# First output projection of a hybrid decoder block: convolution features in seven products, heads plain

## Chip, cores and metric

The kernel runs on one core of one Trainium2 chip. The metric is device microseconds (us) of the whole kernel, lower is better. Three runs of the kernel before gave 2041.8, 2042.85 and 2043.69 us, median 2042.85 us.

## The reference, cut to what matters

One decoder block over 2048 positions of width 1024 in float32: norm, one input projection, two mixers side by side, one output projection with residual, norm, a gated feed-forward part with residual, norm.

```python
proj = rmsnorm(x, norm1_g[l]) @ w_in[l]
p_q, p_k, p_v, p_g, p_a, c_b, c_c, c_h = jnp.split(proj, splits, axis=-1)
...
o = rmsnorm(gla_chunked(q, k, v, log_a), gla_norm_g[l]) 
o_gla = (o * silu(p_g)).reshape(bsz, seq, GLA_WIDTH)
o_conv = c_b * causal_depthwise_conv(c_c * c_h, conv_w[l])
mixed = jnp.concatenate([o_gla, o_conv], axis=-1) @ w_out[l]
x = x + mixed
h2 = rmsnorm(x, norm2_g[l])
x = x + (silu(h2 @ w_ffn_gate[l]) * (h2 @ w_ffn_up[l])) @ w_ffn_down[l]
```

The change lies in `mixed`: a product of 2048 x 1024 features (512 of gated linear attention, here "the heads", and 512 of the convolution) with a 1024 x 1024 matrix.

## The kernel before, in words

**Number format and products.** Features stand on the 128 partitions and positions in the free dimension, in four blocks `b` of 512. Each operand is split into two float32r parts, a high part made by ScalarE (L194) and a low part made by VectorE as the difference (L195); the helper `split` does both. A product step is then three matmuls of 128x512: high by high, high by low, low by high (L484 to L486 in `product_step`).

**Units.** The input projections and the feed-forward part work in units of a 2 x 2 scheme of Strassen and Winograd: two feature halves by two position blocks, seven products in place of eight. The list `PRODUCTS` names them: A11 B11, S1 T1, S2 T2, A12 B21, S3 T3, S4 B22, A22 T4, where the A's, S's are weights or their sums and the B's, T's operands or their differences. The results are accumulated in PSUM banks (`mm`) and by copies (`copied`, ScalarE, L530) and additions (`plus`, VectorE, L518) in tiles of SBUF. The operands T3, B22 and T4 (`WHOLE`) are stored as they are and split only when due, in the middle of a unit (`due`). Weights come raw from DRAM and are split into tiles `wq`, of which there are four buffers.

**Stages.** First input projection (blocks 0 and 1, `in_proj(0)`, to about 270 us), second one (blocks 2 and 3, `in_proj(1)`), then the output projection of blocks 0 and 1 (`out_proj(0)`, about 555 to 663 us) and that of blocks 2 and 3 (`out_proj(1)`), then the feed-forward part, twice. In `in_proj` the last units make the convolution; its result `y` (a tile of the pool `tp`, nine buffers that many purposes share) is split at once, and `hi` and `y` are stored in DRAM (`s_mix`). The recurrence of the heads (`gla_half`) runs as a background generator: `tick`, called between products, takes a step of it, so that its chunks are spread over the second input projection and the first output projection. The last step of a chunk transposes (`ot`, L1231), scales (`osb`, L1232), splits and stores (`s_gla`); the split is put behind the last copy and the last addition recorded (`behind(last_out + last_plus)`). The other generators hang on `tick` too: `ahead` takes a step at one tick in four.

**The output projection.** `out_proj(half, ops)` takes 16 operand pairs (8 k of 128 features by 2 blocks; k 0 to 3 the heads, 4 to 7 the convolution), all loaded ready split by `build_mix`. It makes four passes over `d0`, each for two rows `e` of 128 output features: four banks, and for each k, e and block j three matmuls (L1273, L1274, L1276). Behind a pass, four additions on VectorE of the residual `y` (L1298), four stores, four squares on ScalarE (L1254) and their sums on VectorE (L1255).

**What sets the order.** A scheduler orders the instructions of each engine ahead of time; every engine then takes its queue in order. All loads and stores are issued by SyncE (L148 and L151) in one order, and each DMA also waits for the landing of the eighth before it, since there are eight lanes. The operand pool `opp` has 28 buffers.

Of the kernel before, what the change touches and what calls it, by code (L numbers as in the profile page):

```python
# [16 lines left out]
ALU = mybir.AluOpType  # L17
# [36 lines left out]
def tile_hymba_block(ctx, tc, x, xt, win, wa, wgu, wout, wffn, wdown, wdown_first, small, out):  # L54
# [59 lines left out]
    s_mix = [[dram.tile([P, 2, PB], F32, name=f"sm{b}_{k}") for k in range(4)] for b in range(NB)]  # L114
    s_gla = [dram.tile([P, HEADS, 2, PB], F32, name=f"sgla{b}") for b in range(NB)]
    s_act = [
        [
# [279 lines left out]

    def weight_quarter(src):

        n = src.shape[-1]  # L400
# [7 lines left out]
        split(src, h[:, 0, :], h[:, 1, :])  # L408
        catch_up()
        return h  # L410

# [5 lines left out]
        return raw  # L417

    def unit_weights(src, raw=None, between=()):
        raw = raw_weights(src) if raw is None else raw  # L420
# [6 lines left out]
        n = src.shape[-1]  # L427
        a11, a12, a22, a21 = [raw[:, i, :] for i in range(4)]
        s1 = rawp.tile([P, PB], F32, name="s1", tag="s1", bufs=1)[:, 0:n]
# [24 lines left out]
        return w  # L454
# [585 lines left out]
    def forget_gate(b, i, z, em, dn, el):  # L1040
# [15 lines left out]
        dve.tensor_tensor(dn[:, i, :], em[:, i, :], el[:, i, :], ALU.mult)  # L1056
        store(s_d[b][i][:], t2[:])

    def in_proj(half, ops, raw=None, between=(), rest=None):
        def units():  # L1060
            if half == 0:
# [15 lines left out]
        for i0 in (0, 2):  # L1077
# [179 lines left out]
    def build_mix(half):  # L1257
        def pair(b, k):
            return load_pair(s_gla[b][:, k] if k < HEADS else s_mix[b][k - HEADS])

        return [[pair(2 * half + j, k) for j in range(2)] for k in range(KD)]

    def out_proj(half, ops, ahead=None, rest=None):
        ssq = []
        ws = chain.from_iterable(plain_weights(wout[u], 4) for u in range(4))
        for d0 in range(0, KD, 2):
            o = {(e, j): bank() for e in range(2) for j in range(2)}
            for k in range(KD):
                for e in range(2):
                    wh, wl = next(ws)  # L1270
                    for j in range(2):
                        m = ops[k][j]
                        pe.matmul(o[e, j][:], wh, m[:, 0, :], start=k == 0, stop=False)  # L1273
                        pe.matmul(o[e, j][:], wh, m[:, 1, :], start=False, stop=False)  # L1274
                    for j in range(2):
                        pe.matmul(  # L1276
                            o[e, j][:], wl, ops[k][j][:, 0, :], start=False, stop=k == KD - 1
                        )
# [6 lines left out]
                if half:  # L1285
                    for _ in range(1 if d0 == KD - 2 else 2):
                        next(rest if d0 == KD - 2 else ahead, None)
                tick()
            if d0 == 0:
                ssq += [  # L1290
# [391 lines left out]
    in_proj(0, ops, raw, between, rest)  # L1682
    drain_background()
    ops = load_pairs(s_h1)
    background.extend([pause(3), hastened(gla_half(0), 14), gate(1, ops)])
# [5 lines left out]
    ssq = out_proj(1, build_mix(1), h2_first(ssq, h2), h2_rest(h2))  # L1691
    ahead.append(h2_ahead(ssq))
    mixing.close()
    bx[:] = [
# [112 lines left out]
```

## Time and profile before

| | |
|---|---|
| median of three runs | 2042.85 us |
| the profiled execution's own time | 2040.97 us |
| its span | 2039.2 us |
| TensorE busy in the span | 2019.6 us, 99% |
| VectorE, ScalarE busy | 1534.0 us (75%), 966.0 us (47%) |
| bytes moved | 422.51 MB, 207 GB/s in the mean |

A timeline row gives the start and the duration in us, engine, line, operation, destination <- source, the shape and the count; in brackets the idle time of the engine ahead of it and what ended that. PEld are TensorE's weight loads, SPq is SyncE's issuing queue. A row of windows gives the stretch, its length, then busy us and count for PE, PEld, VectorE (DVE), ScalarE (ACT) and POOL, the granted TensorE clock, the DMA share and GB/s. A row of waits gives engine, tile and line, what it waited for, and the total, the count and the longest in us. Group rows end with the idle time ahead of the group and what ended it.

### The profile page before, as it was taken

What the parts mean: (1) busy time and instruction counts of PE and PEld (TensorE: products, weight loads), DVE (VectorE), ACT (ScalarE), POOL (GpSimd) and SP (SyncE); (2) the same over time, 40 slices, a digit from 0 to 9 for tenths busy, and PEclk for the clock granted to TensorE, in tenths of its full rate; (3) what the DMA queues carried; (4) which work ended last, traced back from release to release, by engine and by line L of the source; (5) the groups of instructions that cost most, each with busy time, mean ns of one, the idle gap of its engine ahead of it and who ended that gap; (6) DMA issues with size and microseconds to landing.
All of it is one profiled execution on the core that took longest, in us unless ns stands there. A gap on an engine that the chain in (4) does not pass through costs nothing.

```text
span 2039.2 us, 26918 instructions
## 1 busy us (share of the span) xinstructions
PE 2019.6 (99%) x9299; PEld 1659.4 (81%) x9299; DVE 1534.0 (75%) x2763; ACT 966.0 (47%) x1915; POOL 10.3 (1%) x17
## 2 busy tenths in 40 slices
PE   9999999999999999999999999999999999999998
PEld 8788877887888788888888888887888888888886
DVE  7888967659744697777777688887777767778886
ACT  6664455656533344444444452334534444454345
POOL 0000000000000000000000000000000000000001
PEclk9999999999999999999999999999999999999999
DMA  7356885524675983546545576577444434486653
GB/s 263 119 202 222 290 299 172 163 74 158 247 245 173 373 293 134 192 151 217 181 145 191 215 287 249 187 276 279 161 165 170 161 144 170 174 331 223 248 217 129
DMA packets 190887, 422.51 MB, mean 207 GB/s; under 512 B 20032, under 2 KB 67360, under 8 KB 181280
## 3 DMA queue, kind: packets, MB, share of 16 engines
q1 hardware_dynamic: 190032, 420.15, 58.2%
q8 instruction: 73, 1.20, 0.2%
q10 hardware_dynamic: 720, 0.66, 0.1%
q14 instruction: 62, 0.51, 0.1%
HBM read 276.02 MB, written 144.70 MB: 206 GB/s over the span
## 4 chain that ended last, share of the span: by engine, by line
PE 94%; DMA 2%; DVE 2%; ACT 1%; issue 0%; SPq 0%; POOL 0%; POOLq 0%; ACTq 0%; DVEq 0%
PE mm L484 26%; PE mm L486 26%; PE mm L485 26%; PE mm L1273 3%; PE mm L1274 3%; PE mm L1276 3%; PE a_ps L1008 1%; PE mm L789 1%; PE mm L791 1%; PE o_ps L1181 1%; PE mm L790 1%; PE mm L1594 1%; PE sc L1156 1%; PE o_ps L1188 1%; DMA op<-shT 0%; PE kv L1196 0%
## 5 line engine op out<-in xcount | busy, mean ns | idle before, releaser
L484 PE MATMUL mm<-op,wq 128*128 128x512 f32 x2443 | 951.4, 392 | 7.2 <-ACT op L194 4.1
L485 PE MATMUL mm<-op,wq 128*128 128x512 f32 x2443 | 950.2, 390 | 0.5 <-DVE op L195 0.5
L486 PE MATMUL mm<-op,wq 128*128 128x512 f32 x2443 | 940.5, 390 | 0.3
L194 ACT ACTIVATE wq<-raw 128x512 fp32r<-128x512 f32 (+2 forms) x612 | 356.8, 588 | 590.1 <-PE mm L486 469.9
L484 PEld LDWEIGHTS mm<-op,wq 128*128 128x128 f32 x2443 | 459.0, 188 | 108.8 <-ACT op L194 5.4
L486 PEld LDWEIGHTS mm<-op,wq 128*128 128x128 f32 x2443 | 458.9, 188 | 96.5 <-DVE wq L195 1.1
L485 PEld LDWEIGHTS mm<-op,wq 128*128 128x128 f32 x2443 | 459.1, 188 | 96.1 <-DVE op L195 2.4
L195 DVE TENSOR_TENSOR wq<-raw,wq 128x512 fp32r<-128x512 f32 (+2 forms) x612 | 385.4, 635 | 173.5 <-ACT wq L194 171.9
L518 DVE TENSOR_TENSOR c<-mm,c 128x512 f32<-128x512 f32 x196 | 134.7, 687 | 81.6 <-PE mm L486 72.0
L518 DVE TENSOR_TENSOR y<-mm,y 128x512 f32<-128x512 f32 x185 | 126.6, 687 | 53.8 <-PE mm L486 53.2
L530 ACT ACTIVATE c<-mm 128x512 f32<-128x512 f32 x198 | 115.4, 589 | 34.7 <-PE mm L486 30.6
L436 DVE TENSOR_TENSOR raw<-raw 128x512 f32<-128x512 f32 (+2 forms) x182 | 113.3, 628 | 2.1
L194 ACT ACTIVATE wq<-s 128x512 fp32r<-128x512 f32 (+2 forms) x96 | 56.3, 587 | 108.8 <-PE mm L486 95.7
L1273 PE MATMUL mm<-op,wq 128*128 128x512 f32 x256 | 101.1, 397 | 0.1
L1274 PE MATMUL mm<-op,wq 128*128 128x512 f32 x256 | 100.0, 391 | 0.0
L1276 PE MATMUL mm<-op,wq 128*128 128x512 f32 x256 | 82.3, 390 | 0.0
L436 DVE TENSOR_TENSOR s<-raw 128x512 f32<-128x512 f32 (+2 forms) x91 | 57.3, 629 | 27.3 <-DMA raw<-in_wffn_dram 19.7
L195 DVE TENSOR_TENSOR op<-op 128x512 fp32r<-128x512 f32 x94 | 62.1, 683 | 4.0 <-ACT op L194 3.9
L195 DVE TENSOR_TENSOR wq<-s,wq 128x512 fp32r<-128x512 f32 (+2 forms) x96 | 60.8, 633 | 1.9 <-ACT wq L194 1.0
L194 ACT ACTIVATE op<-op 128x512 fp32r<-128x512 f32 x94 | 54.9, 621 | 8.0 <-DMA op<-sa_T 4.3
L436 DVE TENSOR_TENSOR raw<-s,raw 128x512 f32<-128x512 f32 (+2 forms) x91 | 57.3, 630 | 1.3
L1273 PEld LDWEIGHTS mm<-op,wq 128*128 128x128 f32 x256 | 48.1, 188 | 11.8 <-issue 1.4
(231 smaller groups left out, 1610.2 us busy)
## 6 DMA issues: line engine op xcount, KB each, us to landing
raw<-in_wffn_dram SPq DMA_DIRECT2D x44, 1024.0 KB, 6.4
sa_B<-so SPq DMA_DIRECT2D x47, 512.0 KB, 4.2
op<-sa_B SPq DMA_DIRECT2D x47, 512.0 KB, 6.8
raw<-in_win_dram SPq DMA_DIRECT2D x22, 1024.0 KB, 5.8
sa_T<-so SPq DMA_DIRECT2D x44, 512.0 KB, 4.4
op<-sa_T SPq DMA_DIRECT2D x44, 512.0 KB, 6.7
raw<-in_wdown_dram SPq DMA_DIRECT2D x24, 768.0 KB, 5.4
sx<-y SPq DMA_DIRECT2D x48, 256.0 KB, 3.9
```

The lines of the kernel that those rows point to most:

```text
L194: last_hi[:] = [act.activation(hi, src, AF.Copy)]
L195: last_lo[:] = [dve.tensor_tensor(lo, src, hi.bitcast(F32), ALU.subtract)]
L436: dve.tensor_tensor(*args)
L484: pe.matmul(o[:], wh, xh, start=first and k == 0, stop=False, skip_group_check=True)
L485: pe.matmul(o[:], wh, xl, start=False, stop=False, skip_group_check=True)
L486: return pe.matmul(o[:], wl, xh, start=False, stop=k == n - 1, skip_group_check=True)
L518: last_plus[:] = [dve.tensor_tensor(t[:], o[:], t[:], ALU.add)]
L530: last_out[:] = [act.activation(t[:], o[:], AF.Copy)]
L789: pe.matmul(acc[:], wq[:, 0, c], p[:, 0, :], start=first, stop=False)
L1273: pe.matmul(o[e, j][:], wh, m[:, 0, :], start=k == 0, stop=False)
L1274: pe.matmul(o[e, j][:], wh, m[:, 1, :], start=False, stop=False)
L1276: pe.matmul(o[e, j][:], wl, ops[k][j][:, 0, :], start=False, stop=k == KD - 1)
```

## The change

Only the first output projection (blocks 0 and 1) and what feeds it:

- `s_mix` of blocks 0 and 1 is stored whole; the split into `hi` and `y` falls away there (in the second half it stands as before, as `pair_out`).
- A new generator `conv_operands` hangs on `ahead` during the second input projection. After four pauses it takes, for each of two k, five steps: load four blocks of `s_mix` into small tiles, make four differences, split B11, T1, B21 and T2 and store both parts, store T3 and T4 whole, in new tiles of DRAM (`s_conv`).
- `mix_operands` loads 14 operands of the convolution (8 pairs, 6 whole) and 8 pairs of the heads.
- `first_out_proj` takes the place of `out_proj(0)`. Per pass it makes the weights of seven products of 256 columns (`unit_weights` with four quarters given: seven splits and four sums and differences) and two splits of 512 for the heads, then seven products of two product steps with an addition after each use, then the heads' matmuls, those of e = 0, j = 0 on top of the bank of A12 B21, and four additions. The rows of the residual are loaded a pass ahead.
- `out_proj` keeps the second output projection alone.

```diff
-                hi = tp.tile([P, PB], F32R, name="hi", tag="t")
-                split(y[:], hi[:], y[:].bitcast(F32R))
                 dst = s_mix[2 * half + j][i0 + r]
-                store(dst[:, 0, :], hi[:].bitcast(F32))
-                store(dst[:, 1, :], y[:])
+                if half:
+                    pair_out(y, dst)
+                else:
+                    store(dst[:], y[:])
...
+    def conv_operands():
...
+        yield from pause(4)
+
+        def divided(y, n, k):
+            with behind(last_out + last_plus):
+                pair_out(y, s_conv[n][k])
+
+        for k in range(2):
...
+            for y, src in (
+                (b11, s_mix[0][k]), (b12, s_mix[1][k]), (b22, s_mix[1][k + 2]), (b21, s_mix[0][k + 2]),
+            ):
+                load(y[:], src[:])
+            yield
+            t3 = tt("t3")
+            subtract(t3, b22, b12)
+            store(s_conv["T3"][k][:], t3[:])
+            subtract(b12, b12, b11)
+            divided(b11, "B11", k)
+            yield
+            subtract(b22, b22, b12)
+            divided(b12, "T1", k)
+            yield
...
+        for d0 in range(0, KD, 2):
+            raw = raw_weights(wout[d0 // 2]).rearrange("p a (b e c) -> p (a b) e c", e=2, c=P)
+            quads = [raw[:, k : k + 2, e, :] for e, k in ((0, 4), (0, 6), (1, 6), (1, 4))]
+            w = unit_weights(None, quads)
+            wh = [weight_quarter(raw[:, 0:HEADS, e, :]) for e in range(2)]
...
+            def plus(at, o):
+                last_plus[:] = [dve.tensor_tensor(y[at][:], o[:], y[at][:], ALU.add)]
+                last_out[:] = last_plus
+                all_plus.extend(last_plus)
+
+            oa = mul(0)
+            plus((0, 0), oa)
+            ob = mul(1)
+            plus((1, 1), ob)
+            due("T3")
+            tick()
+            mul(2, oa)
+            plus((0, 1), oa)
+            due("B22")
+            o = mul(3)
+            tick()
+            mul(4, oa)
+            plus((1, 1), oa)
+            due("T4")
+            mul(5, ob)
+            plus((0, 1), ob)
+            tick()
+            mul(6, oa)
+            plus((1, 0), oa)
+            tick()
+            following = residual(d0 + 2) if d0 + 2 < KD else None
+            for e in range(2):
+                po = [bank() if e or j else o for j in range(2)]
+                for k in range(HEADS):
+                    c = slice(k * P, (k + 1) * P)
+                    for j in range(2):
+                        for part in range(2):
+                            pe.matmul(
+                                po[j][:], wh[e][:, 0, c], heads[k][j][:, part, :],
+                                start=k + part == 0 and e + j > 0, stop=False,
...
-    ssq = out_proj(0, build_mix(0))
+    ssq = first_out_proj(residual(0), *mix_operands())
```

**Where instructions move.** ScalarE's order at the boundary of the two input projections, before; `hi` are the convolution's high parts, c11, c22 and c12 the copies of the last unit's results, the last row the first split of T3:

```order
L194 ACTIVATE hi_2816<-c22_2412 128x512
L194 ACTIVATE hi_2822<-c12_2437 128x512
L194 ACTIVATE wq_2901<-raw_2889 128x512
L194 ACTIVATE wq_2904<-raw_2889 128x512
L194 ACTIVATE hi_2828<-c11_2507 128x512
L530 ACTIVATE c11_2920<-mm_2907 128x512
L194 ACTIVATE wq_2922<-raw_2889 128x512
L530 ACTIVATE c22_2939<-mm_2926 128x512
L194 ACTIVATE wq_2941<-raw_2889 128x512
L530 ACTIVATE c12_2956<-mm_2907 128x512
L194 ACTIVATE wq_2958<-raw_2889 128x512
L194 ACTIVATE op_2865<-op_2865 128x512
```

The same place with the change, where L198 is the line of `split` and L542 that of the copies:

```order
L542 ACTIVATE c11_2902<-mm_2889 128x512
L198 ACTIVATE wq_2883<-raw_2871 128x512
L198 ACTIVATE wq_2886<-raw_2871 128x512
L198 ACTIVATE wq_2904<-raw_2871 128x512
L542 ACTIVATE c22_2921<-mm_2908 128x512
L198 ACTIVATE wq_2923<-raw_2871 128x512
L542 ACTIVATE c12_2938<-mm_2889 128x512
L198 ACTIVATE wq_2940<-raw_2871 128x512
L198 ACTIVATE op_2847<-op_2847 128x512
```

The three `hi` rows are gone and the copies come in the same order; c22 and c12 waited there for lanes of DMAs beside TensorE, and with the change wait for TensorE alone.

ScalarE's order at the end of the first output projection, before; `gt<-osb` is the high part of the last chunk of the heads, the `wq` are weights of the second output projection:

```order
L1213 ACTIVATE sq_6548,hsq_6545<-o_ps_6536 128x128
L200 ACTIVATE hl_6546<-hsq_6545 128x4
L201 ACTIVATE hy_6547<-hl_6546 128x4
L194 ACTIVATE wq_6746<-raw_6717 128x512
L194 ACTIVATE gt_6296<-osb_6559 128x512
L194 ACTIVATE wq_6803<-raw_6717 128x512
L1254 ACTIVATE q_6663<-y_6589 128x512
```

The same place with the change (`q` are the squares, L1272):

```order
L198 ACTIVATE wq_6669<-raw_6641 128x512
L205 ACTIVATE hy_6718<-hl_6717 128x4
L1272 ACTIVATE q_6791<-y_6536 128x512
L198 ACTIVATE wq_6873<-raw_6871 128x512
L198 ACTIVATE wq_6900<-raw_6871 128x512
L1272 ACTIVATE q_6796<-y_6540 128x512
L198 ACTIVATE gt_6448<-osb_6730 128x512
L198 ACTIVATE wq_6957<-raw_6871 128x512
```

Two weight splits and two squares now stand between the row of `hy` and the head's split, where one weight split stood; `wq_6900` takes the buffer of `wq_6663`, the weights of the last product.

TensorE's order at that place with the change: `ot` are the last chunk's transposes, mm_6672 the bank of the last product (weights `wq_6663`), mm_6799 and mm_6800 the heads' banks:

```order
L1249 MATMUL ot_6754<-ident_87,osb_6730 128x128 x3
L1386 MATMUL mm_6799<-op_5790,wq_6669 128x512 x2
L1386 MATMUL mm_6800<-op_5792,wq_6669 128x512 x2
L1392 MATMUL mm_6799<-op_5790,wq_6669 128x512
L1392 MATMUL mm_6800<-op_5792,wq_6669 128x512
L1386 MATMUL mm_6799<-op_5794,wq_6669 128x512
L496 MATMUL mm_6672<-op_5786,wq_6663 128x512
L497 MATMUL mm_6672<-op_5786,wq_6663 128x512
L498 MATMUL mm_6672<-op_5786,wq_6663 128x512
L496 MATMUL mm_6672<-op_5788,wq_6663 128x512
L497 MATMUL mm_6672<-op_5788,wq_6663 128x512
L498 MATMUL mm_6672<-op_5788,wq_6663 128x512
```

Between these transposes and the first matmul that reads the last chunk (`op_6837`, in the second output projection) stand 33 matmuls of 128x512, 13 of them up to the end of the last product; before, 41 stood between the transposes and that first use.

More of the change, by code (lines that the diff above doesn't have):

```diff
@@ L407, in weight_quarter @@
             h = h[:, :, 0:n]
-        split(src, h[:, 0, :], h[:, 1, :])
+        hi, lo = h[:, 0, :], h[:, 1, :]
+        if not whole:
+            hi, lo = [y.rearrange("p (k c) -> p k c", c=P) for y in (hi, lo)]
+        split(src, hi, lo)
         catch_up()
@@ new lines, in mix_operands, with residual @@
+    def mix_operands():
+        for _ in ahead.pop():
+            pass
+        s_conv["B22"] = s_mix[1][2:4]
+        ops = no_operands()
+        for _, n in PRODUCTS:
+            ops[n] = [(load_undivided if n in WHOLE else load_pair)(p) for p in s_conv[n]]
+            if n in WHOLE:
+                undivided[n] = ops[n]
+        return ops, [[load_pair(s_gla[j][:, k]) for j in range(2)] for k in range(HEADS)]
+    def residual(d0):
+        y = {}
+        for i, (r, j) in enumerate(((0, 0), (1, 1), (0, 1), (1, 0))):
+            if d0 or i > 1:
+                y[r, j] = tt("y")
+            else:
+                y[r, j] = tiny.tile([P, PB], F32, name="y", tag="rb")
+            load(y[r, j][:], xt[j, :, d0 + r, :])
+        return y
@@ new lines, in first_out_proj, with mul @@
+    def first_out_proj(y, conv, heads):
+        ssq = [
+            tiny.tile([P, PB], F32, name=f"ssx{j}", tag=f"ssx{j}", bufs=1) for j in range(2)
+        ]
+        for d0 in range(0, KD, 2):
[3 more added lines that the diff above has]
+            wh = [weight_quarter(raw[:, 0:HEADS, e, :]) for e in range(2)]
+            def mul(i, o=None):
+                first = o is None
+                o = bank() if first else o
+                n, m = PRODUCTS[i]
+                for k in range(2):
+                    product_step(o, w[n], conv[m], k, first)
+                return o
+            def plus(at, o):
[32 more added lines that the diff above has]
+                                start=k + part == 0 and e + j > 0, stop=False,
+                                skip_group_check=True,
+                            )
+                    for j in range(2):
+                        pe.matmul(
+                            po[j][:], wh[e][:, 1, c], heads[k][j][:, 0, :], start=False,
+                            stop=k == HEADS - 1, skip_group_check=True,
+                        )
+                    if k % 2:
+                        tick()
+                for j in range(2):
+                    plus((e, j), po[j])
+                    store(s_x1[j][d0 + e][:], y[e, j][:])
+                    sum_squares(ssq[j], y[e, j][:], d0 + e == 0)
+            y = following
+        return ssq
@@ L1284, in out_proj @@
                             load(ys[e, j][:], xt[2 * half + j, :, d0 + e, :])
-                if half:
-                    for _ in range(1 if d0 == KD - 2 else 2):
-                        next(rest if d0 == KD - 2 else ahead, None)
+                for _ in range(1 if d0 == KD - 2 else 2):
+                    next(rest if d0 == KD - 2 else ahead, None)
                 tick()
```

51 lines of the change are left out of this document (40 added, 11 removed).

## The prediction

> **What bounds the kernel now.** I read the page's busy shares first, then its chain of waits, then the list of what TensorE waited for, and last the timelines of the stretches that the change touches.
>
> ```profile
> PE 2019.6 (99%) x9299; PEld 1659.4 (81%) x9299; DVE 1534.0 (75%) x2763; ACT 966.0 (47%) x1915; POOL 10.3 (1%) x17
> PE 94%; DMA 2%; DVE 2%; ACT 1%; issue 0%; SPq 0%; POOL 0%; POOLq 0%; ACTq 0%; DVEq 0%
> PE mm L484 <- ACT op L194: 4.1, 2, 2.3
> ```
>
> TensorE is busy for 2019.6 of 2039.2 us and makes up 94% of the chain that ended last. So time goes only with matmuls taken out of TensorE's queue or with its few waits, and comes only with new waits or a lower clock. The change therefore has two sides: fewer matmuls, and whether every neighbour still delivers in time.
>
> **What one matmul is worth.** The timeline of TensorE inside the first output projection:
>
> ```profile
> 557.66 0.39 PE L1273 MATMUL mm<-op,wq 128*128 128x512 f32 x1
> 557.89 0.39 PE L1274 MATMUL mm<-op,wq 128*128 128x512 f32 x1
> 558.12 0.39 PE L1273 MATMUL mm<-op,wq 128*128 128x512 f32 x1
> 558.34 0.39 PE L1274 MATMUL mm<-op,wq 128*128 128x512 f32 x1
> 558.57 0.39 PE L1276 MATMUL mm<-op,wq 128*128 128x512 f32 x1
> ```
>
> The second column says 0.39 us, but the first column steps by (558.57 - 557.66) / 4 = 0.227 us: matmuls overlap, and taking one out frees 0.227 us, not 0.39. Before, a pass issues 8 k x 2 e x 2 j x 3 = 96 matmuls; now 7 products x 2 k x 3 = 42 for the convolution features and 4 x 2 x 2 x 3 = 48 for the heads, 90. Over 4 passes 24 go: 24 x 0.227 = **-5.4 us**.
>
> **The boundary of the two input projections.** The longest TensorE waits that the change touches, with ScalarE's and SyncE's rows:
>
> ```profile
> 261.52 0.39 SPq L151 DMA_DIRECT2D sm<-hi  x1
> 265.14 0.32 SPq L151 DMA_DIRECT2D sm<-c  x1
> 268.99 0.60 ACT L530 ACTIVATE c<-mm 128x512 f32<-128x512 f32 x1 [3.46 <-PE mm L486]
> 269.48 0.62 ACT L194 ACTIVATE wq<-raw 128x512 fp32r<-128x512 f32 x1
> 269.90 0.39 PE L486 MATMUL mm<-op,wq 128*128 128x512 f32 x1
> 270.93 0.60 ACT L530 ACTIVATE c<-mm 128x512 f32<-128x512 f32 x1 [0.83 <-DMA sm<-c]
> 271.42 0.62 ACT L194 ACTIVATE wq<-raw 128x512 fp32r<-128x512 f32 x1
> 272.61 0.50 PE L484 MATMUL mm<-op,wq 128*128 128x512 f32 x1 [2.32 <-ACT op L194]
> 273.43 0.50 PE L485 MATMUL mm<-op,wq 128*128 128x512 f32 x1 [0.31 <-DVE op L195]
> 274.47 0.63 PE L486 MATMUL mm<-op,wq 128*128 128x512 f32 x1
> 277.87 0.40 PE L485 MATMUL mm<-op,wq 128*128 128x512 f32 x1
> 1398.43 0.50 PE L484 MATMUL mm<-op,wq 128*128 128x512 f32 x1 [1.78 <-ACT op L194]
> 274.00:276.00 2.00, 2.00 (x7) 1.61 (x6) 2.00 (x4) 2.00 (x5) 0.00 (x0) 0.61 1.04 354
> 1398.00:1402.00 4.00, 3.34 (x13) 2.44 (x14) 3.57 (x6) 3.63 (x7) 0.00 (x0) 1.00 1.00 336
> ```
>
> The copy of c12 at 270.93 waits for its buffer until a store of the convolution's output has landed; behind it on ScalarE stand a weight split and the splits of T3, for which TensorE waits 2.32 us. The change removes the `hi` tiles and their stores; in the order the copy then waits for TensorE alone. ScalarE's copy of c22 at 268.99 waits for a buffer in the same way in the order, for the `hi` store. With both free, c12 follows its product's end near 269.0 (four matmuls before the row of 269.90), its weight split at 269.5, T3's first `hi` runs from 270.05 to 270.7 and TensorE goes on near 270.8 instead of 272.61: 1.8 us, and 0.2 of the second wait. After the wait the clock falls: from 274.47 to 277.87 eight matmuls take 3.40 us where eight at 0.227 take 1.82, so 1.6 us at a granted clock of 0.61; the wait of 1.78 us at 1398.43 left the clock at 1.00, so a shorter one may spare that. The gain lies between 0 (the transfers, at a DMA share of 1.04, are still late and hold another buffer) and 1.8 + 0.2 + 1.6 = 3.6. I take **-3.0**, near the upper end, because the row named as the copy's releaser, `sm<-c`, loses the store that went ahead of it.
>
> **What is added in the second input projection.** Eight subtractions, eight ScalarE and eight VectorE halves of splits, eight loads and some 20 stores, against eight halves on each engine gone earlier.
>
> ```profile
> 440.00:500.00 60.00, 58.78 (x268) 47.23 (x267) 46.72 (x90) 34.81 (x74) 0.00 (x0) 1.00 0.40 129
> 460.00:480.00 20.00, 19.67 (x87) 15.96 (x86) 20.00 (x41) 16.02 (x36) 0.00 (x0) 1.00 0.35 107
> PE mm L484 <- ACT c L530: 0.9, 1, 0.9
> ```
>
> Over 440 to 500 us VectorE has 13 us free and the DMA share is 0.40, so the work fits beside the matmuls; only 460 to 480 is full (20.00 of 20.00), and there a few more rows of 0.69 us come ahead of a copy that TensorE already waits 0.9 us for. Between that wait gone (-0.9) and three such rows in its way (+2.1) I take **+0.5**.
>
> **Operands and VectorE in the first output projection.** Twenty-two operand tiles are loaded where there were sixteen, the convolution's ahead of the heads':
>
> ```profile
> 540.00:560.00 20.00, 20.00 (x105) 15.82 (x104) 15.70 (x32) 9.86 (x25) 0.00 (x0) 1.00 1.03 407
> 560.00:660.00 100.00, 100.00 (x540) 81.54 (x539) 48.49 (x109) 37.77 (x106) 0.00 (x0) 1.00 0.66 213
> L518 DVE TENSOR_TENSOR c<-mm,c 128x512 f32<-128x512 f32 x196 | 134.7, 687 | 81.6 <-PE mm L486 72.0 <-ACT wq L194 4.8 <-ACT c L530 2.4
> L195 DVE TENSOR_TENSOR op<-op 128x512 fp32r<-128x512 f32 x94 | 62.1, 683 | 4.0 <-ACT op L194 3.9
> L195 DVE TENSOR_TENSOR wq<-raw,wq 128x256 fp32r<-128x256 f32 x48 | 19.2, 419 | 5.5 <-ACT wq L194 5.4
> 900.00:1000.00 100.00, 100.00 (x443) 82.81 (x442) 79.33 (x125) 45.75 (x80) 0.00 (x0) 1.00 0.53 188
> ```
>
> Transfers fill the window from 540 to 560 (share 1.03, 407 GB/s). The bytes are 8 x 0.5 + 6 x 0.25 MB for the convolution and 8 x 0.5 for the heads, 9.5 MB against 8: 1.5 MB more is 3.7 us at 407 GB/s. But the heads are first needed some 42 matmuls (9.5 us) after the convolution, so between 0 and 3 us of this shows; I take **+0.7**.
>
> VectorE gets 24 more additions (24 x 0.687 = 16.5), six halves of operand splits (6 x 0.683 = 4.1) and per pass seven splits and four mixes of 256 columns for two splits of 512 fewer (4 x (11 x 0.419 - 2 x 0.687) = 12.9): 33.5 us, from 48.5 in 100 us to 82 in 94.6, 87%. The window 900 to 1000 carries 79% with TensorE never idle. But here a bank is written again only six matmuls (1.36 us) after its addition became possible, three times a pass: an addition (0.69) hides unless one or two other rows stand ahead of it. Between 0 and 12 x 0.42 = 5 us (two ahead at each, 3 x 0.69 - 1.36 = 0.7, with half of it covered by recurrence matmuls standing between) I take **+1.6**.
>
> **The hand-over to the second output projection.** Its first step reads the last chunk of the heads, which still has to be scaled, split, stored and loaded:
>
> ```profile
> 654.88 0.49 PE L1231 MATMUL ot<-ident,osb 128*128 128x128 f32 x3
> 655.40 0.75 DVE L1232 SCALAR_TENSOR_TENSOR osb<-ot,sml,gt 128x512 f32<-128x512 f32 x1 [1.36 <-PE ot L1231]
> 656.19 0.63 ACT L194 ACTIVATE gt<-osb 128x512 fp32r<-128x512 f32 x1 [2.88 <-DVE osb L1232]
> 657.57 0.51 SPq L151 DMA_DIRECT2D sgla<-osb  x1
> 658.62 0.63 ACT L194 ACTIVATE wq<-raw 128x512 fp32r<-128x512 f32 x1 [1.80 <-PE mm L1276]
> 660.32 3.70 SPq L148 DMA_DIRECT2D op<-sgla  x7
> 664.32 0.39 PE L1276 MATMUL mm<-op,wq 128*128 128x512 f32 x1
> 664.79 0.47 PE L1273 MATMUL mm<-op,wq 128*128 128x512 f32 x1
> ```
>
> From the transposes' end (655.1) to the use at 664.79 is 9.7 us, 7.2 of them from the store's issue at 657.57. TensorE covered this with 41 matmuls (9.3 us) and was held for 664.79 - 664.32 - 0.23 = 0.24 us: the chain is already critical. Now the order leaves 33 matmuls in between, 7.5 us. Besides, on ScalarE the split of weights `wq_6900` stands ahead of the split of `osb`, and the row at 658.62 shows what such a weight split does: it waits for the matmuls that still read its buffer (1.80 us). Here these are those of the last product, 13 matmuls = 2.95 us after the transposes. Weight split 0.63, a square 0.61, the head's split 0.63 and its second half 0.69 put the store 5.6 us after the transposes instead of 2.45. So 5.6 + 7.2 - 7.5 = 5.3 us of waiting in place of 0.24: +5.0. If the buffer is free early, 2.45 + 7.2 - 7.5 = 2.2, so +1.9. For the clock after such a wait I add 1.3 of the 1.6 measured above: **+6.3**, between +1.9 and +7.
>
> The Trainium skill, "TensorE: Matmul & The Clock Gate", section "HAM oscillation — how this bites in real kernels", warns of idle gaps over about 3.4 us, behind which the array runs at half clock for another such window. The trace agrees only in part: 2.32 + 0.31 us of idle already gave 0.61. By the page the boundary's dip would not be the wait's, and its term would be -2.0, and the hand-over's +6.6: +2.0 in all.
>
> **The sum.** -5.4 - 3.0 + 0.5 + 0.7 + 1.6 + 6.3 = +0.7 us on the profiled execution of 2040.97 us (span 2039.2 and 1.8 around it). The runs' median lies 1.9 above that, so 2042.85 + 0.7 = **2043.6 us**. Faster or slower by 0.2% means 4.1 us, about what a measurement can tell from none: below 2038.8 or above 2046.9.
>
> **The rivals.**
>
> *Faster: the hand-over holds little.* If the buffer of `wq_6900` is free early, the term is +1.9 without a clock dip, 4.4 less: 2039.2; with the passes and the loads at nothing 2.3 less again, 2036.9. For it speaks that the weights' splits are short; against it that the head's split stands behind them in an in-order queue. Chance 0.22, at the middle of the two, 2038.0.
>
> *Slower: VectorE sets the pace of the passes.* At twelve places, three a pass, a bank is written again after 1.36 us. If a weight split and a mix stand ahead of each addition, each costs 0.7 us without help: 8.4 instead of 1.6, and 2050.4. It decides when VectorE, at 87% on average, is a row and a half behind in the passes that also carry recurrence work. For it speaks the full stretch 460 to 480, where TensorE waited; against it the window 900 to 1000. Chance 0.28.
>
> *The saving is 24 x 0.39 = 9.4 us*, 2039.6: the steps of 0.227 us speak against it, and it lies within the forecast's case.
>
> That the matmuls are not saved is excluded by the order: it has exactly 24 fewer.
>
> **How the numbers follow.** The forecast has 0.5, and 2039 to 2047 is its own range. The range with both others reaches from 2036.5 to 2050.5. Faster 0.22, same 0.5, slower 0.28.
>
> **What would show it.** The boundary: the wait at L484 for ScalarE's `op` near 270 us is gone and the clock stays at 1.00. The hand-over: a wait of some 5 us for `op<-sgla` ahead of the second output projection's first heads. The passes: waits of the new matmuls for VectorE's `y`, under 2 us in all. It is wrong if the hand-over's wait is under 2 us, if the stall at the boundary moves to another buffer, or if VectorE's waits are over 5 us.

## The result, and the profile after

The changed kernel takes 2047.16 us (median of 13 runs, 2043.54 to 2052.74), the kernel before 2042.68 us (13 runs, 2039.73 to 2043.94). The ratio is 1.0025 with an interval of 1.0016 to 1.0033: **slower by 0.25%**, 3.3 to 6.7 us. The forecast was 2043.6 us with a range of 2036.5 to 2050.5.

The profiled execution of the changed kernel took 2047.66 us; its span of 2045.9 us is 6.7 us longer than before. From its page the busy shares and the chain, and from its list of TensorE's waits three rows:

```profile
PE 2021.6 (99%) x9275; PEld 1658.7 (81%) x9275; DVE 1563.3 (76%) x2837; ACT 973.5 (48%) x1941; POOL 10.3 (1%) x17
PE 89%; DMA 5%; DVE 3%; ACT 2%; issue 1%; SPq 1%; POOL 0%; POOLq 0%; DVEq 0%; ACTq 0%
```

```profile
PE mm L1421 <- DMA op<-sgla: 4.5, 1, 4.5
...
PE o_ps L1199 <- ACT c L542: 2.1, 1, 2.1
...
PE v_ps L1183 <- issue: 1.4, 1, 1.4
```

The 2.32 us of the boundary for ScalarE's `op` is gone from the list. New are 4.5 us for the heads' operand, 2.1 us for the recurrence's outputs (`o_ps`) and 1.4 us for a transpose (`v_ps`). To see how much each stretch gained or lost, take four events that both kernels have, and compare their starts. TensorE's timeline before: the last product for the gates, transposes of a chunk, the first matmul of the second output projection and its last rows.

```profile
467.26 0.40 PE L1034 MATMUL z<-a_sb,wgu_sb 96*128 96x512 f32 x1
...
513.95 0.60 PE L1231 MATMUL ot<-ident,osb 128*128 128x128 f32 x4
...
663.86 0.39 PE L1273 MATMUL mm<-op,wq 128*128 128x512 f32 x1
...
752.95 0.62 PE L1276 MATMUL mm<-op,wq 128*128 128x512 f32 x2
```

The same four after:

```profile
464.57 0.40 PE L1046 MATMUL z<-a_sb,wgu_sb 96*128 96x512 f32 x1
...
515.01 0.60 PE L1249 MATMUL ot<-ident,osb 128*128 128x128 f32 x4
...
665.57 0.39 PE L1421 MATMUL mm<-op,wq 128*128 128x512 f32 x1
...
760.91 0.62 PE L1424 MATMUL mm<-op,wq 128*128 128x512 f32 x2
```

The differences are -2.7, +1.1, +1.7 and +8.0 us. Each stretch's share is the step from one to the next:

| stretch | forecast, us | measured, us |
|---|---|---|
| up to the gates' product (boundary of the input projections) | -3.0 | -2.7 |
| up to the chunk's transposes (end of the second input projection) | +0.5 | +3.8 |
| up to the second output projection | -5.4 + 0.7 + 1.6 = -3.1 | +0.7 |
| through the second output projection (hand-over) | +6.3 | +6.2 |
| everything behind that | 0 | -1.3 |
| sum | +0.7 | +6.7 |

Most of the last difference is a wait that the change does not touch: 1.78 us at 1398 us before, 0.78 us at 1405 us after. The table is that of one execution of each kernel; the medians lie 4.5 us apart and not 6.7.

**The boundary.** ScalarE and TensorE, after:

```profile
266.88 0.60 ACT L542 ACTIVATE c<-mm 128x512 f32<-128x512 f32 x1 [1.60 <-PE mm L498]
...
274.40 0.63 ACT L198 ACTIVATE wq<-raw 128x512 fp32r<-128x512 f32 x1 [1.93 <-DMA raw<-in_win_dram]
275.08 0.50 PE L496 MATMUL mm<-op,wq 128*128 128x512 f32 x1 [1.02 <-ACT wq L198]
```

The copy waits for TensorE alone, as the order said, and no operand's high part holds TensorE there any more; for a low part it waits 0.23 us at 271 us, where it waited 0.31. What is late next is a load of raw weights: 1.02 us. The granted clock over 274 to 278 us was 1.00 this time.

**The end of the second input projection.** TensorE, then ScalarE and VectorE, after:

```profile
488.18 1.19 PE L1199 MATMUL o_ps<-vt,scores 128*128 128x128 f32 x4 [2.15 <-ACT c L542]
```

```profile
487.55 1.07 ACT L542 ACTIVATE c<-mm 128x512 f32<-128x512 f32 x2
487.60 0.77 DVE L1177 COPY_PREDICATED scores<-mask,sc 128x256 f32<-128x256 uint32 x2
```

The outputs need a bank, which the copy from 487.55 frees, and the masked scores, which VectorE makes only at 487.60. In the order they now stand two matmuls behind that chunk's transposes; before, 24 matmuls stood between. The clock falls while TensorE still waits: read in windows of 0.1 us it is 0.50 from 487.85 to 494.67. TensorE works at half speed from 488.18 to 494.67, 6.5 us, so by an estimate the clock costs 3.2 us on top of the wait. It need not fall: two of the runs below, the convolution first and the weights earlier, have the same wait of 2.15 us at the same place and keep a clock of 1.00. TensorE's row of the run with the convolution first:

```profile
487.77 0.68 PE L1202 MATMUL o_ps<-vt,scores 128*128 128x128 f32 x4 [2.15 <-ACT c L545]
```

From the gates' product to the chunk's transposes these two runs take 47.5 us, the kernel before 46.7 and the changed kernel's trace 50.4. So the wait costs 0.8 us in that stretch, and the other 3 us of the 3.8 are the clock of this execution.

**Inside the first output projection.** VectorE and TensorE at the start of the third pass:

```profile
612.88 0.42 DVE L448 TENSOR_TENSOR s<-raw 128x256 f32<-128x256 f32 x1 [4.26 <-DMA raw<-in_wout_dram]
...
614.94 0.35 DVE L1224 TENSOR_SCALAR kvs<-kv,el 128x128 f32<-128x128 f32 x1
...
615.39 0.63 PE L1183 MATMUL v_ps<-ident,vt 128*128 128x128 f32 x4 [1.39 <-issue]
...
616.36 0.47 PE L496 MATMUL mm<-op,wq 128*128 128x512 f32 x1 [0.33 <-DVE osb L1240]
```

VectorE waits for raw weights with the recurrence's rows behind it in its queue; the transposes start 0.1 us after `kvs` has read the bank `kv`. That this bank is the one they wait for is read from the order of events: the row itself names no releaser.

**The hand-over.** After, ahead of the second output projection:

```profile
658.41 0.49 PE L1249 MATMUL ot<-ident,osb 128*128 128x128 f32 x3
...
659.99 0.64 ACT L198 ACTIVATE gt<-osb 128x512 fp32r<-128x512 f32 x1
...
661.92 0.69 DVE L1355 TENSOR_TENSOR y<-mm,y 128x512 f32<-128x512 f32 x1 [0.76 <-PE mm L498]
662.53 0.68 DVE L199 TENSOR_TENSOR osb<-osb,gt 128x512 fp32r<-128x512 f32 x1
...
663.24 0.52 SPq L155 DMA_DIRECT2D sgla<-osb  x1
...
670.95 0.80 PE L1421 MATMUL mm<-op,wq 128*128 128x512 f32 x1 [4.54 <-DMA op<-sgla]
```

From the transposes' end (658.65) to the second part's store 4.6 us pass, from there to the use 7.7 us; the 33 matmuls cover 7.6 us. The chain's holder is VectorE's addition of the last product at 661.92, which stands ahead of the head's low part. The clock is 0.50 from 668.75 to 675.58; TensorE works at that speed for 4.6 us, an estimated 2.3 us lost. One row of windows behind the wait:

```profile
671.00:675.00 4.00, 4.00 (x10) 3.13 (x11) 0.00 (x0) 0.00 (x0) 0.00 (x0) 0.50 1.00 376
```

### The profile page after: what moved, and what is told of

Same layout as the page of the kernel before. It is cut to its first block, busy times and chain, and to the rows that moved or that the text cites. A ratio compares the mean times of both kernels' runs of the same rounds, so it can differ in the third digit from the quotient of the medians.

```text
span 2045.9 us, 27026 instructions
## 1 busy us (share of the span) xinstructions
PE 2021.6 (99%) x9275; PEld 1658.7 (81%) x9275; DVE 1563.3 (76%) x2837; ACT 973.5 (48%) x1941; POOL 10.3 (1%) x17
## 4 chain that ended last, share of the span: by engine, by line
PE 89%; DMA 5%; DVE 3%; ACT 2%; issue 1%; SPq 1%; POOL 0%; POOLq 0%; DVEq 0%; ACTq 0%
PE mm L496 26%; PE mm L498 26%; PE mm L497 26%; PE mm L1421 1%; PE mm L1424 1%; PE mm L1422 1%; DMA raw<-in_win_dram 1%; DMA op<-shT 1%; PE a_ps L1020 1%; PE mm L801 1%; PE mm L803 1%; PE mm L802 1%; PE mm L1741 1%; PE mm L1386 1%; PE o_ps L1199 1%
## 5 line engine op out<-in xcount | busy, mean ns | idle before, releaser
L496 PE MATMUL mm<-op,wq 128*128 128x512 f32 x2499 | 974.3, 393 | 4.1 <-ACT wq L198 1.5
L497 PE MATMUL mm<-op,wq 128*128 128x512 f32 x2499 | 972.3, 390 | 0.6 <-DVE op L199 0.5
L498 PE MATMUL mm<-op,wq 128*128 128x512 f32 x2499 | 962.1, 390 | 0.3
L198 ACT ACTIVATE wq<-raw 128x512 fp32r<-128x512 f32 (+2 forms) x628 | 361.8, 581 | 599.5 <-PE mm L498 477.6
L496 PEld LDWEIGHTS mm<-op,wq 128*128 128x128 f32 x2499 | 469.5, 188 | 107.6 <-ACT wq L198 4.6
L498 PEld LDWEIGHTS mm<-op,wq 128*128 128x128 f32 x2499 | 469.5, 188 | 99.9 <-DVE wq L199 1.9
L497 PEld LDWEIGHTS mm<-op,wq 128*128 128x128 f32 x2499 | 469.8, 188 | 98.6 <-DVE op L199 2.6
L199 DVE TENSOR_TENSOR wq<-raw,wq 128x512 fp32r<-128x512 f32 (+2 forms) x628 | 389.8, 625 | 165.2 <-ACT wq L198 163.6
L542 ACT ACTIVATE c<-mm 128x512 f32<-128x512 f32 x198 | 115.5, 589 | 33.1 <-PE mm L498 30.6
L198 ACT ACTIVATE wq<-s 128x512 fp32r<-128x512 f32 (+2 forms) x100 | 58.0, 580 | 101.3 <-PE mm L498 91.5
L199 DVE TENSOR_TENSOR op<-op 128x512 fp32r<-128x512 f32 x100 | 66.3, 683 | 3.7 <-ACT op L198 3.5
L198 ACT ACTIVATE op<-op 128x512 fp32r<-128x512 f32 x100 | 59.2, 622 | 9.1 <-DMA op<-siT 3.2
L597 ACT ACTIVATE sg<-mm 128x512 f32<-128x512 f32 x26 | 15.5, 597 | 85.1 <-PE mm L498 85.1
L597 ACT ACTIVATE c<-c 128x512 f32<-128x512 f32 x78 | 48.9, 629 | 13.3 <-DVE c L530 10.6
L1421 PE MATMUL mm<-op,wq 128*128 128x512 f32 x128 | 50.8, 399 | 4.5 <-DMA op<-sgla 4.5
L1422 PE MATMUL mm<-op,wq 128*128 128x512 f32 x128 | 50.5, 395 | 0.0
```

Of the source, the lines that this page charges most:

```text
L198: last_hi[:] = [act.activation(hi, src, AF.Copy)]
L199: last_lo[:] = [dve.tensor_tensor(lo, src, hi.bitcast(F32), ALU.subtract)]
L496: pe.matmul(o[:], wh, xh, start=first and k == 0, stop=False, skip_group_check=True)
L497: pe.matmul(o[:], wh, xl, start=False, stop=False, skip_group_check=True)
L498: return pe.matmul(o[:], wl, xh, start=False, stop=k == n - 1, skip_group_check=True)
L542: last_out[:] = [act.activation(t[:], o[:], AF.Copy)]
```

## The experiments

My theory at this point: the matmuls and the boundary gave what they should, and three waits took it back: the recurrence's outputs near 485 us, queues inside the first output projection, and the hand-over. The rivals: the matmuls are not worth 5.4 us, VectorE's load as such sets the pace, or the waits only move when one is taken away. Each run was compared with the kernel before on its own chip.

**Matmuls alone.** The kernel before, with 24 matmuls fewer in its first output projection:

```diff
                     for j in range(2):
+                        if not half and (k == 4 or (k == 5 and e == 0)):
+                            continue
                         pe.matmul(
                             o[e, j][:], wl, ops[k][j][:, 0, :], start=False, stop=k == KD - 1
```

> The kernel before with 24 matmuls left out of its first output projection (the low-by-high product of k = 4, and of k = 5 at e = 0, in each of the four passes); nothing else is changed. If a matmul is worth the 0.227 us between starts, TensorE's queue gets 5.4 us shorter, but six of the 24 stand between the last chunk's transposes and its first use (41 there before, 35 now), and the hand-over's chain was already critical, so 1.4 us come back as a longer wait for the heads' operand: 4.1 us faster in all, 2038.6 on 2042.7. If the duration of 0.39 us counted, 9.4 us faster. If TensorE did not bound that stage, no change.

Measured: 2038.71 against 2041.8 us, ratio 0.9981 (0.9973 to 0.9990): 3.1 us faster between the medians, 3.9 by the ratio. At the hand-over TensorE was held for 1.63 us between starts (1.47 in the row, which counts from the modelled end), where it was 0.24:

```profile
661.53 0.47 PE L1273 MATMUL mm<-op,wq 128*128 128x512 f32 x1 [1.47 <-DMA op<-sgla]
```

So 0.227 us per matmul holds, 0.39 does not, and what is taken out of the cover of a critical chain comes back: six matmuls there are 1.36 us, and the wait grew by 1.39. From the chunk's transposes to the last row of the second output projection this trace is 2.9 us shorter than that of the kernel before, which is about 5.4 less 1.4 at the hand-over, 0.35 of a new wait for `y`, and some 0.9 where a chunk's 14 small matmuls, in one piece before (632 us), stand in three.

**Storing alone.** The kernel before, with the convolution's output of blocks 0 and 1 stored whole:

```diff
-                hi = tp.tile([P, PB], F32R, name="hi", tag="t")
-                split(y[:], hi[:], y[:].bitcast(F32R))
                 dst = s_mix[2 * half + j][i0 + r]
-                store(dst[:, 0, :], hi[:].bitcast(F32))
-                store(dst[:, 1, :], y[:])
+                if half:
...
+                else:
+                    store(dst[:], y[:])
...
+            if k >= HEADS and not half:
+                return load_whole(s_mix[b][k - HEADS])
```

> The kernel before with only the storing changed: the convolution's output of blocks 0 and 1 is stored whole and split when the first output projection loads it (eight splits more there, eight fewer before the boundary). My theory: the waits of 2.32 and 0.31 us at the boundary shrink as they did in the changed kernel, where the events behind it came 2.7 us sooner, and the eight splits hide beside the output projection's matmuls: 2.7 us faster, 2040.0. The rival: from 455 to 490 us VectorE is full, so that coming there 2.7 us sooner only makes TensorE wait longer there: 0 us, and a wait of some 3 us near 485 us in place of 0.9.

Measured: 2037.55 against 2041.8 us, ratio 0.9980 (0.9971 to 0.9989), 4.1 us faster. In the trace 3.3 us of it are there at the gates' product, so the boundary gave more than the 2.7 expected. Its waits are two small ones:

```profile
271.27 0.50 PE L488 MATMUL mm<-op,wq 128*128 128x512 f32 x1 [0.48 <-DVE op L198]
275.62 0.50 PE L489 MATMUL mm<-op,wq 128*128 128x512 f32 x1 [0.67 <-DVE wq L198]
```

Near 485 us TensorE waits 0.90 us for a copy, as before (0.89). So arriving earlier at the stretch where VectorE is full is not what makes the wait of 2.15 us: that rival falls.

**The hand-over taken away.** The changed kernel, with the convolution's features first in the second output projection:

```diff
+CONV_FIRST = (4, 5, 6, 7, 0, 1, 2, 3)
...
-        return [[pair(2 + j, k) for j in range(2)] for k in range(KD)]
+        return {k: [pair(2 + j, k) for j in range(2)] for k in CONV_FIRST}
...
-        for i in range(n):
+        for i in (2, 3, 0, 1):
             h = weight_quarter(raw[:, i, :])
...
-            for k in range(KD):
+            for i, k in enumerate(CONV_FIRST):
```

> The changed kernel, with the second output projection taking the convolution's features ahead of the heads (k in the order 4 to 7, 0 to 3), so that 82 matmuls and not 33 stand between the last chunk's transposes and its first use. My theory of the hand-over: the wait of 4.5 us and the lower clock behind it go, 6.3 us less than the changed kernel, about 2041 where that has 2047. The rival, that VectorE's load in the first output projection delays TensorE anyway: another wait takes the place, and the time stays within 2 us of 2047.

Measured: 2040.41 against 2041.8 us, ratio 0.9993 (0.9984 to 1.0002). Next to the changed kernel's 1.0025 that is 0.32%, 6.5 us; the term of 6.2 us is confirmed, and no wait stands at the hand-over: the second output projection takes 88.4 us in this trace, 95.3 in the changed kernel's and 89.1 before. But loads of 512 KB now go ahead of the recurrence's fetches, and a new wait appears:

```profile
612.84 0.30 PE L1186 MATMUL v_ps<-ident,vt 128*128 128x128 f32 x1 [1.70 <-DMA vt<-sv]
```

**The operand steps earlier.**

```diff
-        yield from pause(4)
+        yield from pause(2)
```

> The changed kernel with two pauses ahead of the convolution's operand steps in place of four, so that they end some 20 us earlier and no row of them stands in the stretch from 450 to 490 us where VectorE is full. In the order the recurrence's outputs then stand 24 matmuls behind the transposes of that chunk again, as before the change, not two. My theory: the wait of 2.15 us near 485 us and the clock of 0.53 behind it came from that, and go: 3 us less than the changed kernel, 2044. The rival: the wait comes because TensorE arrives 2.7 us earlier at a stretch that VectorE bounds; then waits of the same sum stand there, and the time stays at 2047.

Measured: 2043.73 against 2041.8 us, ratio 1.0010 (1.0001 to 1.0018): 0.15% or 3.1 us less than the changed kernel. The wait of 2.15 us and the low clock are gone; TensorE's longest there is again the old one:

```profile
487.64 0.50 PE L496 MATMUL mm<-op,wq 128*128 128x512 f32 x1 [0.85 <-ACT c L542]
```

From the gates' product to the chunk's transposes the trace takes 46.7 us, as before the change and 3.7 less than the changed kernel's. Of these 0.8 us is the wait and the rest is the clock, which differs from one execution to the next. The run does two things at once, takes a VectorE row of the operand steps (0.68 us) out of the full stretch and brings the old order of the recurrence back, and does not tell their shares apart.

**Weights earlier.**

```diff
+            if d0 + 2 < KD:
+                fetched = raw_weights(wout[d0 // 2 + 1])
             following = residual(d0 + 2) if d0 + 2 < KD else None
```

> The changed kernel with the raw output weights of each pass fetched ahead of the residual rows of that pass in program order, where the change fetched them behind. In the changed kernel VectorE waited 4.26 us at 613 us for raw<-in_wout, the additions of the recurrence's state stood behind that, and TensorE waited 1.39 and 0.33 us for banks. My theory: that wait of VectorE goes, and 1.9 us with it: 2045. The rival: VectorE's queue is full with the additions of seven products anyway, and TensorE's waits in the first output projection keep their sum: 2047.

Measured: 2046.31 against 2042.1 us, ratio 1.0019 (1.0010 to 1.0028), which does not differ from the changed kernel's. This one is inconclusive: the load of the third pass kept its place in SyncE's order, VectorE still waited 3.8 us for it, and TensorE's wait stayed:

```profile
611.09 0.63 PE L1183 MATMUL v_ps<-ident,vt 128*128 128x128 f32 x4 [1.38 <-issue]
```

**Two edits, and three.** The convolution first and the earlier steps together; then these with the edit on the weights.

> The changed kernel with the edits of the two runs before together: operand steps two pauses earlier, and the convolution ahead of the heads in the second output projection. If the two waits are independent, the gains of 3.1 and 6.5 us measured apart add: 2047.2 - 9.6 = 2037.6, which is about the kernel before with only the storing changed (2037.5). If one wait only moves into the other's place, not under 2040.

Measured: 2039.93 against 2042.1 us, ratio 0.9986 (0.9977 to 0.9995): 0.39% less than the changed kernel, 8.0 us, and not the full 9.6. The waits that are left:

```profile
PE v_ps L1186 <- DMA vt<-sv: 1.7, 1, 1.7
...
PE mm L1389 <- DMA op<-sgla: 1.1, 1, 1.1
```

> As the run before, and the output weights fetched ahead of the residual rows as well. If the late weights cost 1.9 us in the changed kernel independently of the rest, 2035.7, the fastest of all; if that wait is gone already by the other order of the recurrence that the earlier steps bring, the same as the run before, 2037.6.

Measured: 2037.96 against 2042.1 us, ratio 0.9982 (0.9973 to 0.9992). Its interval overlaps that of the run before, so nothing is settled on the late weights.

**Loads behind the fetch.** The two edits, with the second output projection's loads put behind the last fetch of the recurrence:

```diff
-        return {k: [pair(2 + j, k) for j in range(2)] for k in CONV_FIRST}
+        with behind(last_fetch):
+            return {k: [pair(2 + j, k) for j in range(2)] for k in CONV_FIRST}
```

> The kernel of the run with earlier steps and the convolution first, with the loads of the second output projection's operands put behind the last fetch of the recurrence in SyncE's queue, where six loads of 512 KB had gone ahead of two of its fetches. TensorE's order is then that of the run with earlier steps up to the hand-over. My theory: the waits of 1.7 us for vt<-sv, 1.1 us for the heads' operand and 0.8 us near 594 us came from those loads in SyncE's queue and go, so the gains of 3.1 and 6.5 us add after all: 2037.6, 4.6 us under the kernel before. The rival: they come from VectorE's load, and the time stays at 2039.9.

Measured: 2036.45 against 2042.0 us (6 runs, 2035.26 to 2037.56), ratio 0.9970 (0.9959 to 0.9981). It is 5.5 us under the kernel before between the medians, and 0.55% under the changed one: the sum of the two gains (0.47%) is reached. The waits for `vt<-sv` and near 594 us (0.78 us) are gone from the trace; 1.1 us for `v_ps`, 1.4 in the changed kernel, and 0.7 us for `op<-sgla` remain. The interval overlaps that of the two edits alone (0.9977 to 0.9995), so what the place of the loads is worth is not settled by the times.

> The kernel before with only the storing changed, once more, on the same chip as the run above, to weigh the seven products themselves: if their 24 matmuls fewer are worth 5.4 us less what VectorE and the loads take back in that stage (3.5 us in the run with earlier steps), the run above is 2 us under this one; if the stage gives all of them back, the two are equal within 1 us.

Measured on the same chip: 2038.12 against 2042.0 us (11 runs), ratio 0.9982 (0.9973 to 0.9991). The version with seven products has the lower median by 1.7 us, but the two intervals overlap (0.9959 to 0.9981 and 0.9973 to 0.9991), and the traces do not put the difference down to the products. From the chunk's transposes to the last row of the second output projection, where all of the products stand, it takes 751.19 - 512.25 = 238.9 us with them:

```profile
512.25 0.60 PE L1252 MATMUL ot<-ident,osb 128*128 128x128 f32 x4
...
751.19 0.62 PE L1428 MATMUL mm<-op,wq 128*128 128x512 f32 x2
```

With the storing alone it is 749.33 - 510.50 = 238.8 us, and 239.0 in the kernel before:

```profile
510.50 0.60 PE L1237 MATMUL ot<-ident,osb 128*128 128x128 f32 x4
...
749.33 0.62 PE L1284 MATMUL mm<-op,wq 128*128 128x512 f32 x2
```

So in these traces the stage gives the 5.4 us back even with both waits mended. The four slowest of the eleven runs with the storing alone have a mean clock of 0.997, all six of the other version 0.998, so part of the 1.7 us is the clock; where the rest comes from is open.

## Why the prediction was right or wrong

**Matmuls: right.** 24 x 0.227 us; the run with 24 fewer bears out the size and the 1.4 us that a critical chain takes back.

**Boundary: right.** -2.7 for -3.0. The waits gave 1.4 us (2.32 + 0.31 became 0.23 + 1.02) and not 2.0; the low clock from 274.43 to 277.84, which was worth 1.7, is gone and made up for it. What is late next is a load of raw weights that the sum did not have: the stall did move in part to another buffer, which the prediction had named as a sign of being wrong.

**Second input projection: the mechanism failed, and the clock was left out.** It had "a few more rows of 0.69 us" ahead of a copy and took +0.5, with 2.1 as its upper end; 3.8 came in the profiled execution, but 0.8 in the two runs with the same wait at full clock, which is inside its bounds. It counted VectorE's rows and not what the scheduler makes of them elsewhere: the recurrence's outputs moved from 24 matmuls to two behind their chunk's transposes, in front of VectorE's full queue. That row of the order was there to be read. The low clock behind the wait cost an estimated 3.2 us more in this execution, a price that the step did not carry.

**First output projection: the step failed in size.** Loads and VectorE were to cost 0.7 + 1.6 = 2.3 us; the stretch lost 0.7 + 5.4 = 6.1. The mechanism named for it, additions of the seven products that come too late for the bank, is not in the list of waits: no product waits for `y`. So the rival "VectorE sets the pace" did not come about either. In its place stand, by the rows, 0.44 us for the heads' operand, 1.39 + 0.33 us behind the late weights, and a cost that no wait shows. One chunk's outputs in one piece, before, and in two pieces, after:

```profile
603.50 0.62 PE L1276 MATMUL mm<-op,wq 128*128 128x512 f32 x2
603.96 1.05 PE L1181 MATMUL o_ps<-vt,scores 128*128 128x128 f32 x8
...
606.18 0.50 PE L1273 MATMUL mm<-op,wq 128*128 128x512 f32 x1
```

```profile
602.42 0.40 PE L1392 MATMUL mm<-op,wq 128*128 128x512 f32 x1
602.65 0.61 PE L1199 MATMUL o_ps<-vt,scores 128*128 128x128 f32 x4
...
604.67 0.50 PE L496 MATMUL mm<-op,wq 128*128 128x512 f32 x1
...
605.93 0.39 PE L498 MATMUL mm<-op,wq 128*128 128x512 f32 x1
606.25 0.49 PE L1206 MATMUL o_ps<-carry,kq 64*128 64x128 f32 x2
...
607.25 0.73 PE L1386 MATMUL mm<-op,wq 128*128 128x512 f32 x2
```

In one piece it takes 606.18 - 603.50 - 2 x 0.227 = 2.2 us out of the matmuls' row; in two, (604.67 - 602.42 - 0.23) + (607.25 - 605.93 - 0.23) = 3.1. Summed in this way from about 540 us to the second output projection, the recurrence's pieces take 21.2 us before, 25.8 after and 23.8 in the run with earlier steps: about 2.6 us for the broken order alone, and 2.0 for the waits at 615. Another 0.8 us is of the same kind: the second matmul behind a piece starts 0.34 us after the first and not 0.227 (604.67 and 605.01), at 17 places after and 10 before. With the 0.44 for the heads' operand nearly all of the 6.1 is named. That breaking the groups is the cause was read, not tested by a run of its own; the kernel before shows the same on a small scale, with a chunk's 14 small matmuls in 1.37 us in one piece (611.5) and in 2.06 in three (590.0 to 593.4).

**Hand-over: right in time, partly by luck.** +6.2 for +6.3, and the run that puts the convolution first takes it away. But the wait grew by 4.4 us between starts and not by 5.0, and the clock cost an estimated 2.3 and not 1.3; the two errors cancel. And ScalarE's weight split `wq_6900` did not hold the head's split, and the sentence in the section on the change that it takes the last product's buffer is wrong: it waited for the heads' first weights and was through by 659.3. VectorE's addition of the last product was the holder. The store came 4.6 us behind the transposes and not 5.6, and the transfer took 7.7 us and not 7.2.

**The forecast as a whole.** 2043.6 against 2047.16 us lies in the range, but by its bound of 0.2% "about the same" was the wrong case by 0.05%, which is less than the interval (0.16 to 0.33%) can tell. The medians moved by 4.5 us where 0.7 was forecast: in the profiled execution two terms were too small by 3.3 and 3.8 us, and the case "slower", at 0.28, came by other roads than its own.

**The clock.** Forecast was 1.3 us for one dip; there were two, of an estimated 3.2 and 2.3 us, where the kernel before has one of 1.7. The Trainium skill, "TensorE: Matmul & The Clock Gate", section "What's actually happening", says that the activity window is free-running. The runs agree: in the changed kernel's trace the clock is low from 487.85 to 494.67 and from 668.75 to 675.58, with 174.08 us between, and in that with the weights' edit from 612.23 to 615.65 and from 666.85 to 673.67, with 51.20 between; all of these are whole multiples of 3.413 us. Laid on steps of 3.413 us counted from there, each wait is cut in its own way. The same wait of 2.15 us, in the changed kernel and then in the run with the convolution first, two steps each:

```profile
484.43:487.85 3.42, 1.52 (x8) 0.85 (x8) 3.42 (x8) 3.42 (x9) 0.00 (x0) 1.00 0.84 277
487.85:491.26 3.41, 3.08 (x10) 2.56 (x11) 3.41 (x8) 1.14 (x4) 0.00 (x0) 0.50 0.45 173
```

```profile
483.60:487.02 3.42, 1.94 (x16) 1.15 (x12) 3.42 (x7) 3.34 (x8) 0.00 (x0) 1.00 0.86 279
487.02:490.43 3.41, 2.66 (x14) 2.23 (x15) 3.41 (x9) 1.56 (x5) 0.00 (x0) 1.00 0.58 220
```

In the first TensorE is idle for 3.42 - 1.52 = 1.90 us of one step, and the next step runs at 0.50; in the second the wait falls into two steps, with 1.48 and 0.75 us idle, and the clock stays. The pair of waits at the third pass, 1.39 + 0.33 us in the changed kernel and 1.38 + 0.33 in the run with the weights' edit, shows it again, with 1.59 and 1.71 us idle in a step:

```profile
614.14:617.55 3.41, 1.82 (x9) 1.47 (x10) 3.38 (x13) 1.90 (x6) 0.00 (x0) 1.00 0.69 210
617.55:620.96 3.41, 3.41 (x18) 2.82 (x17) 3.41 (x9) 2.89 (x7) 0.00 (x0) 1.00 0.70 231
```

```profile
608.82:612.23 3.41, 1.70 (x15) 1.16 (x14) 3.38 (x15) 1.52 (x5) 0.00 (x0) 1.00 1.07 351
612.23:615.65 3.42, 3.42 (x9) 2.67 (x9) 3.42 (x8) 2.10 (x5) 0.00 (x0) 0.50 0.62 210
```

In the eleven traces up to 2020 us, no step at full clock with at most 1.59 us idle is followed by a low one, and of the nine with 1.70 us or more eight are (the ninth has 1.71). So what counted here is whether a wait puts about half a step of idle time, some 1.7 us, into one step, and that is chance for a wait of 2 us. This was read from the traces and not tested by a run made for it.

It also makes the time differ from run to run. The changed kernel's 13 runs spread over 9.2 us; the mean clock is 0.996 in the four fastest and 0.994 in three of the four slowest, and 0.002 of 2046 us is about 4 us. The kernel before spread over 4.2 us in 13 runs and 7.9 in 33 on another chip.

## What to carry to other kernels

On an engine that is 99% busy, matmuls taken out are worth the spacing of their starts, and only where nothing else is critical beside them: count the cover of each hand-over before and after, since fewer matmuls are also less cover. Read the whole order around a new step, not only the rows that it adds: two of the costs were old instructions that the scheduler moved, the recurrence's outputs in front of a full queue and its groups broken into pieces. Do not price a low clock from one trace: the same wait lowered it in one execution and not in two others. And test the parts of a change alone: here the storing by itself gained 4 us, and even with two waits mended the seven products took as long in their own stage as the plain ones.

## What the runs showed of the hardware that was not expected

A wait of some 2 us can lower the granted clock to 0.50 for one or two steps of 3.41 us: 2.15 us at 488 us did so for 6.83 us in the changed kernel's trace and not at all in two others, 1.38 + 0.33 us did so for 3.41 us in one run and 1.39 + 0.33 not in another. By the traces here it takes about 1.7 us of idle time within one step. Breaking a group of 128-wide matmuls in two between 128x512 ones went with 0.9 us more on TensorE without any wait in the profile (3.1 against 2.2 us).
